# Loads of b issued from ScalarE's queue in a batched matrix product

## The chip, the cores and the metric

The kernel runs on one core of a Trainium2 chip. The time is device time in microseconds of one execution; the median over runs counts. The core has five engines that each take their instructions in order: PE (TensorE, matmuls and transposes), DVE (VectorE), ACT (ScalarE), POOL (GpSimd) and SP (SyncE). Transfers between HBM and on-chip memory are started by an instruction in the stream of one of these engines and carried out by the core's 16 DMA engines, while the engine that started them goes on. Where an instruction has to wait for something, all that stands behind it in the same engine's stream waits with it.

## The reference

```python
batch, m, k, n = 16, 512, 512, 512
a: (batch, m, k) float32      b: (batch, n, k) float32
return np.matmul(a, b.transpose(0, 2, 1)).astype(np.float32)
```

For each of 16 batches, out = a times b transposed, all 512 by 512 in float32. Each matrix is 1 MiB: the kernel must read 32 MiB and write 16 MiB.

## The kernel before

The function `load` (lines 43 to 48) brings in one batch: all of a[i] in one DMA (L46) and all of b[i] in another (L47). Each lays a matrix on 128 partitions, four whole rows on each, 8 KiB in one piece per partition. Six buffers exist for a and six for b. The loads of the first five batches are issued ahead of the loop (AHEAD = 5).

The loop then does the following for each batch i, in this order:

- `halve` (L52): VectorE casts a, then b, from float32 to bf16, one instruction each.
- `turn` (L62, L67): TensorE transposes the 128 by 128 blocks of the bf16 matrix, 16 for a and 16 for b, into PSUM, in groups of eight; each group is copied to SBUF by one instruction, so two copies a matrix. For a the copies run on ScalarE, for b on VectorE.
- `multiply` (L75, L80): for each of four row blocks, TensorE adds up four matmuls of 128 by 128 by 512 in PSUM, and ScalarE copies the block to the output tile `o_sb`, of which there are five buffers.
- `store` (L87): one DMA of 1 MiB writes the output of the batch.
- `load` of batch i + 5, as long as there is one.

All DMAs are started by SP, in program order: ten loads, then store 0, a5, b5, store 1, a6, b6, and so on to store 10, a15, b15, and then stores 11 to 15. The block stands under `tc.manual_schedule()`: each engine's stream has the order of the program text. The language's tile layer puts in all waits: for data, for a buffer to come free, and for the completion counters of the DMAs. So a store waits in SP's stream for ScalarE's last copy of the batch, and the loads behind it in the text wait with it.

ScalarE's stream holds, for each batch, the two copies of the transposed a and then the four copies of the output.

Of the kernel before, what the change touches and what calls it, by code (L numbers as in the profile page):

```python
# [1 line left out]

# [5 lines left out]


@with_exitstack  # L10
def kernel(
    ctx: ExitStack,
    tc: tile.TileContext,
    a: bass.AP,
    b: bass.AP,
    out: bass.AP,
):
    nc = tc.nc
    P = 128
    batch, M, K = a.shape  # L20
    _, N, _ = b.shape
    J = M // P
    KO = K // P
    f32 = mybir.dt.float32
    bf16 = mybir.dt.bfloat16
    AHEAD = 5

    const = ctx.enter_context(tc.tile_pool(name="ident", bufs=1))
    ident = const.tile([P, P], bf16)
    make_identity(nc, ident)  # L30

    apool = ctx.enter_context(tc.tile_pool(name="a_pool", bufs=6))
    bpool = ctx.enter_context(tc.tile_pool(name="b_pool", bufs=6))
    hpool = ctx.enter_context(tc.tile_pool(name="h_pool", bufs=2))
    tpool = ctx.enter_context(tc.tile_pool(name="t_pool", bufs=2))
    opool = ctx.enter_context(tc.tile_pool(name="o_pool", bufs=5))
    tppool = ctx.enter_context(tc.tile_pool(name="tp_pool", bufs=4, space=bass.MemoryType.PSUM))
    ppool = ctx.enter_context(tc.tile_pool(name="p_pool", bufs=4, space=bass.MemoryType.PSUM))

    def load(i):
        a_sb = apool.tile([P, J, K], f32, tag="a")
        b_sb = bpool.tile([P, J, K], f32, tag="b")
        nc.sync.dma_start(a_sb[:], a[i].rearrange("(p j) k -> p j k", j=J))  # L46
        nc.sync.dma_start(b_sb[:], b[i].rearrange("(p j) k -> p j k", j=J))  # L47
        return a_sb, b_sb

    def halve(src, tag):  # L50
        half = hpool.tile([P, J, K], bf16, tag="h" + tag)
        nc.vector.tensor_copy(out=half[:], in_=src[:])  # L52
        return half

    def turn(half, tag, copy):

        turned = tpool.tile([P, KO, J * P], bf16, tag="t" + tag)
        for ko in range(0, KO, 2):
            tp = tppool.tile([P, 2, J * P], bf16, tag="tp")
            for h in range(2):  # L60
                for j in range(J):
                    nc.tensor.transpose(  # L62
                        tp[:, h, j * P:(j + 1) * P],
                        half[:, j, (ko + h) * P:(ko + h + 1) * P],
                        ident[:],
                    )
            copy(out=turned[:, ko:ko + 2, :], in_=tp[:])  # L67
        return turned

    def multiply(aT, bT):  # L70
        o_sb = opool.tile([P, J, N], f32, tag="o")
        for j in range(J):
            ps = ppool.tile([P, N], f32, tag="p")
            for ko in range(KO):
                nc.tensor.matmul(  # L75
                    ps[:], aT[:, ko, j * P:(j + 1) * P], bT[:, ko, :],
                    start=(ko == 0), stop=(ko == KO - 1),
                )

            nc.scalar.copy(  # L80
                out=o_sb[:, j, :].rearrange("m (p j) -> m p j", j=J),
                in_=ps[:].rearrange("m (j p) -> m p j", j=J),
            )
        return o_sb

    def store(i, o_sb):
        nc.sync.dma_start(out[i].rearrange("(p j) n -> p j n", j=J), o_sb[:])  # L87

    loaded = {}
    with tc.manual_schedule():  # L90
        for i in range(min(AHEAD, batch)):
            loaded[i] = load(i)
        for i in range(batch):
            a_sb, b_sb = loaded.pop(i)
            a_h = halve(a_sb, "a")
            b_h = halve(b_sb, "b")
            aT = turn(a_h, "a", nc.scalar.copy)
            bT = turn(b_h, "b", nc.vector.tensor_copy)
            o_sb = multiply(aT, bT)
            store(i, o_sb)  # L100
            if i + AHEAD < batch:
                loaded[i + AHEAD] = load(i + AHEAD)


# [1 line left out]
_INS = ['a', 'b']  # L106
_OUTS = [((16, 512, 512), 'float32')]


# [23 lines left out]
```

## Time and profile before

| | |
|---|---|
| median of 7 runs | 126.63 us (126.42 to 126.82) |
| profiled execution | 126.72 us |
| its span, first to last instruction | 124.8 us |
| busy: TensorE | 92.2 us |
| busy: ScalarE | 68.4 us |
| busy: VectorE | 59.2 us |
| moved | 50.46 MB, mean 404 GB/s |
| HBM read, written | 33.55 MB, 16.78 MB |
| one 1 MiB DMA, issue to landing, median | 19.6 us |

How to read the lines that follow. On the page, the span is cut into 40 equal slices of 3.12 us; a digit is the busy share of a slice in tenths, and the row GB/s is what the DMA engines moved in it. A line of the waits reads: engine and line, what it waited for, then the total in us, the number of times and the longest. "SPq" is the stream of SP, which starts the DMAs. A line of a timeline reads: start in us, duration in us, engine, line, operation, out<-in, number of instructions merged, and in brackets the idle time before it and what ended that. A line of the chain reads: start, duration, what. A line of the windows reads: the stretch, its length, busy time and instructions of PE, PEld (weight loads), DVE, ACT and POOL, the granted TensorE clock, the DMA engines' busy share and GB/s.

### The profile page before, as it was taken

To read this page: it belongs to the slowest core of one execution; us is meant where nothing else is said; L and a number is where in the kernel's file an instruction comes from. 1 tells how busy PE (TensorE), PEld (TensorE's weight loads), DVE (VectorE), ACT (ScalarE), POOL (GpSimd) and SP (SyncE) were. 2 spreads that over 40 slices of the span, in tenths; PEclk is the share of its full clock that TensorE was granted. 3 is DMA by queue.
4 is the path that set the end of the run, shared out by engine and by line. 5 is a ranking of instruction groups with operands and counts; after the bars stand their busy time and mean duration, and the time that the engine had idled before them with its cause. 6 is when DMAs were issued, how large, how long until landed. Compare 5 with 4: busy or idle time off the path is not lost.

```text
span 124.8 us, 1885 instructions
## 1 busy us (share of the span) xinstructions
PE 92.2 (74%) x754; PEld 55.8 (45%) x768; DVE 59.2 (47%) x64; ACT 68.4 (55%) x97; POOL 0.7 (1%) x6
## 2 busy tenths in 40 slices
PE   0069989898989878949586794958769495886900
PEld 0056465655647445534534453444445344444300
DVE  0256555647373564474446537444653645456000
ACT  4041576777768683745738275582826649173610
POOL 2000000000000000000000000000000000000000
PEclk9999999999999999999999999999999999999995
DMA  3999999989999999999999999999999999999982
GB/s 100 425 425 425 423 436 420 412 326 415 436 431 423 423 420 425 436 423 420 425 423 428 428 431 412 423 428 431 428 428 412 428 425 431 428 423 417 417 347 116
DMA packets 6921, 50.46 MB, mean 404 GB/s; under 512 B 768, under 2 KB 768, under 8 KB 768
## 3 DMA queue, kind: packets, MB, share of 16 engines
q1 hardware_dynamic: 6912, 50.33, 96.5%
q8 instruction: 6, 0.10, 0.3%
q14 instruction: 3, 0.02, 0.0%
HBM read 33.55 MB, written 16.78 MB: 403 GB/s over the span
## 4 chain that ended last, share of the span: by engine, by line
DMA 80%; DVE 6%; PE 5%; SPq 3%; issue 1%; ACT 0%; DVEq 0%
DMA b_sb<-in_b_dram 80%; DVE half L52 4%; PE ps L75 3%; PE tp L62 2%; DVE turned L67 2%; SPq L46 1%; SPq L47 1%; ACT o_sb L80 0%; DVEq L52 0%
## 5 line engine op out<-in xcount | busy, mean ns | idle before, releaser
L75 PE MATMUL ps<-turned 128*128 128x512 bf16 x242 | 59.8, 382 | 6.1 <-DVE turned L67 5.5
L80 ACT COPY o_sb<-ps 128x512 f32<-128x512 f32 x64 | 37.5, 586 | 44.0 <-PE ps L75 40.8
L62 PE MATMUL tp<-ident,half 128*128 128x128 bf16 x512 | 34.8, 225 | 20.1 <-DVE half L52 20.1
L62 PEld LDWEIGHTS <-half 128*128 128x128 bf16 x512 | 31.3, 101 | 25.6 <-DVE half L52 24.1
L75 PEld LDWEIGHTS <-turned 128*128 128x128 bf16 x256 | 25.0, 98 | 36.5 <-issue 10.7
L67 ACT COPY turned<-tp 128x1024 bf16<-128x1024 bf16 x32 | 30.8, 1015 | 5.9 <-PE tp L62 5.9
L52 DVE CAST half<-a_sb 128x2048 bf16<-128x2048 f32 x16 | 19.6, 1224 | 22.1 <-DMA a_sb<-in_a_dram 22.1
L67 DVE COPY turned<-tp 128x1024 bf16<-128x1024 bf16 x32 | 20.7, 686 | 19.2 <-PE tp L62 19.2
L52 DVE CAST half<-b_sb 128x2048 bf16<-128x2048 f32 x16 | 19.6, 1226 | 14.7 <-DMA b_sb<-in_b_dram 14.7
L67 ACT ACT_TABLE_LOAD x1 | 1.3, 1283 | 0.7 <-PEq L117 0.7
masks.py:199 POOL TENSOR_SCALAR_AFFINE_SELECT ident<-ident 128x128 bf16<-128x128 bf16 x1 | 0.3, 294 | 0.1
masks.py:197 POOL MEMSET ident<- 128x128 bf16 x1 | 0.2, 205 | 0.3 <-POOLq L117 0.3
L117 POOL MEMSET const-bfloat16-1.0<- 128x1 bf16 x1 | 0.1, 102 | 0.0
L117 POOL MEMSET const-uint8-127<- 128x1 uint8 x1 | 0.1, 102 | 0.0
L117 POOL MEMSET const-float32-0.0<- 128x1 f32 x1 | 0.1, 99 | 0.2 <-issue 0.2
L117 POOL MEMSET const-float32-1.0<- 128x1 f32 x1 | 0.1, 99 | 0.0
## 6 DMA issues: line engine op xcount, KB each, us to landing
a_sb<-in_a_dram SPq DMA_DIRECT2D x16, 1024.0 KB, 19.6
b_sb<-in_b_dram SPq DMA_DIRECT2D x16, 1024.0 KB, 19.6
out_dram<-o_sb SPq DMA_DIRECT2D x16, 1024.0 KB, 19.6
```

Of the source, the lines that this page charges most:

```text
L46: nc.sync.dma_start(a_sb[:], a[i].rearrange("(p j) k -> p j k", j=J))
L47: nc.sync.dma_start(b_sb[:], b[i].rearrange("(p j) k -> p j k", j=J))
L52: nc.vector.tensor_copy(out=half[:], in_=src[:])
L62: nc.tensor.transpose(tp[:, h, j * P:(j + 1) * P], half[:, j, (ko + h) * P:(ko + h + 1) * P], ident[:],)
L67: copy(out=turned[:, ko:ko + 2, :], in_=tp[:])
L75: nc.tensor.matmul(ps[:], aT[:, ko, j * P:(j + 1) * P], bT[:, ko, :], start=(ko == 0), stop=(ko == KO - 1),)
L80: nc.scalar.copy(out=o_sb[:, j, :].rearrange("m (p j) -> m p j", j=J), in_=ps[:].rearrange("m (j p) -> m p j", j=J),)
L117: nc = _bacc.Bacc("TRN2", target_bir_lowering=False, num_devices=1)
```

## The change

The load of b is started by ScalarE instead of SP. The loads of a and the stores stay on SP.

```diff
     def load(i):
         a_sb = apool.tile([P, J, K], f32, tag="a")
         b_sb = bpool.tile([P, J, K], f32, tag="b")
         nc.sync.dma_start(a_sb[:], a[i].rearrange("(p j) k -> p j k", j=J))
-        nc.sync.dma_start(b_sb[:], b[i].rearrange("(p j) k -> p j k", j=J))
+        nc.scalar.dma_start(b_sb[:], b[i].rearrange("(p j) k -> p j k", j=J))
         return a_sb, b_sb
```

In ScalarE's stream the starts of b0 to b4 stand first, ahead of any copy. After that, the start of b(i+5) stands behind the four output copies of batch i and ahead of the two copies of the transposed a of batch i + 1. In SP's stream each load of a follows directly on the store of the batch, and the next store directly on that.

## The prediction

> **What bounds the kernel now.** I read the page's slices first, then the SP queue's waits, the timeline of SP's issues, ScalarE's timeline, and the windows of the end. The slices:
>
> ```profile
> span 124.8 us, 1885 instructions
> PE 92.2 (74%) x754; PEld 55.8 (45%) x768; DVE 59.2 (47%) x64; ACT 68.4 (55%) x97; POOL 0.7 (1%) x6
> DMA  3999999989999999999999999999999999999982
> GB/s 100 425 425 425 423 436 420 412 326 415 436 431 423 423 420 425 436 423 420 425 423 428 428 431 412 423 428 431 428 428 412 428 425 431 428 423 417 417 347 116
> ```
>
> The transfers bound it: full from the second slice to the last but one. 48 transfers of 1.049 MB at 426 GB/s (the window from 60 to 90 us) take 2.46 us each, 118 us in all. One batch is three transfers, 7.36 us. Next, what SP waits for, and its issues:
>
> ```profile
> SPq L87 <- DMA a_sb<-in_a_dram: 22.7, 11, 2.1
> SPq L46 <- DMA b_sb<-in_b_dram: 18.7, 9, 2.4
> SPq L47 <- DMA out_dram<-o_sb: 18.5, 9, 2.1
> ...
> 5.56 0.33 SPq L46 DMA_DIRECT2D a_sb<-in_a_dram  x1
> 8.08 0.33 SPq L47 DMA_DIRECT2D b_sb<-in_b_dram  x1
> ...
> 72.64 0.34 SPq L87 DMA_DIRECT2D out_dram<-o_sb  x1
> ...
> 92.26 0.33 SPq L47 DMA_DIRECT2D b_sb<-in_b_dram  x1
> ```
>
> Each issue waits for a landing. Call a0, b0, s0 the transfers of batch 0. In program order they are a0 b0 ... a4 b4, then s0 a5 b5, s1 a6 b6, up to s10 a15 b15, then s11 to s15. The ninth issue (a4) starts at 5.56, when a0 lands; the tenth (b4) at 8.08, when b0 lands. b15 starts at 92.26, 19.62 us after s8's issue at 72.64; the median from issue to landing is 19.6. So every transfer waits for the one eight places earlier: a store for an a, a load of a for a b, and **a load of b for the store of two batches before** (b15 for s8, b14 for s7). That is the third line above. Today only SP stands in these waits, and nothing but DMA issues is queued behind them.
>
> ScalarE, and the end:
>
> ```profile
> 39.22 0.59 ACT L80 COPY o_sb<-ps 128x512 f32<-128x512 f32 x1 [0.28 <-PE ps L75]
> 39.72 1.93 ACT L67 COPY turned<-tp 128x1024 bf16<-128x1024 bf16 x2
> ...
> 45.12 0.59 ACT L80 COPY o_sb<-ps 128x512 f32<-128x512 f32 x1 [0.28 <-PE ps L75]
> ...
> 81.58 0.59 ACT L80 COPY o_sb<-ps 128x512 f32<-128x512 f32 x1 [0.28 <-PE ps L75]
> 82.08 1.93 ACT L67 COPY turned<-tp 128x1024 bf16<-128x1024 bf16 x2
> ...
> 114.61 0.59 PE ps L75 x2
> ...
> 118.43 0.59 ACT o_sb L80
> ```
>
> With the data there, a batch takes 5.90 us (39.22 to 45.12, last copies of two batches); TensorE sets that. From a batch's first matmul to its last copy's end it is 4.41 us (114.61 to 119.02). Batch 10 is finished at 82.17, ten microseconds before b15 can be issued, and ScalarE goes straight on to batch 11. That free run is what the change touches. At the end, s15 is issued at 119.02 and the span ends 5.78 us later.
>
> **The change, part by part.** *Removed from SP:* 16 issues of 0.33 us, 5.3 us. SP is no engine of the chain except in the first 4.3 us, where it issues faster than the transfers run; worth nothing.
>
> *The start.* a0 and b0 are issued together. If the queues share the transfers equally, a0 lands with b0 near 8.1 instead of 5.57, and the first products come up to 2.5 us later (nothing, if a0 keeps its place). b4, the tenth transfer, holds ScalarE until b0 lands; the table load of 1.28 us may follow it, while a0 is cast (1.23) and transposed. None of it reaches the end: batches 0 to 5 run at 5.90 against transfers at 7.36 and are ahead for good. I take 0.
>
> *Added to ScalarE:* 16 issues, bounded by SP's rows at 0.33 to 0.91 us. Five come before any work. ScalarE is busy 68.4 of 124.8 us, so the others cost nothing by themselves, except the one in the sum below.
>
> *The wait that moves.* ScalarE takes its instructions in order. The load of b(k+5) stands behind batch k's copies and ahead of batch k+1's two copies of turned a. I take the count of eight to run on in program order over both queues: the profile names a landing as releaser, so the program puts the wait there, not a full queue. Then ScalarE stands until s(k-2) has landed; behind it are turned a of batch k+1, the matmuls that need it, the next store, and behind that store on SP the next load of a. TensorE and VectorE can only prepare one batch.
>
> From its release a batch takes 0.33 (issue) + 1.02 (first turned copy, mean 1015 ns) + 4.41 = 5.8 us. Stores land every 7.36 us while the transfers are full. So in the steady state ScalarE waits about 1.5 us in each batch, the transfers stay full (when s8 lands s9, s10, a14, a15 and others are outstanding), and the page would look alike. But the computing now trails: batch 10 ends 1.5 us before b15's issue instead of ten before.
>
> *The end pays for it.* Call T the issue of b15. Batches 11 to 15 are all still to be computed: 5.8 for batch 11, 4 x 5.90 for 12 to 15 with the operands there, then 5.78 for the last store. Span = T + 5.8 + 23.6 + 5.8 = T + 35.2. After T at most twelve transfers are left, 29.5 us, so these are no longer the limit: the transfers run dry between the last stores.
>
> T is the landing of s8. Served in program order that is 92.26 as now. With its own queue, b13 and b14 (the only later loads of b that can be issued without s8) can pass s8, each 2.46 us: T to 97.2. The other way, b12 could fall behind s8: T = 89.8. I take one passed, 94.7, because the b queue holds fewer transfers than the other and so is drained ahead. Span 94.7 + 35.2 = 129.9. The profiled execution took 126.72 with a span of 124.8, so 1.92 lie around it: 131.8. The median of the runs is 126.63, 0.09 lower: **131.7 us**. The ends: T = 89.8 gives 126.8, program order (92.26) 129.3, two passed 134.2.
>
> The share between the queues is in no row of this trace. The Trainium skill, page "DMA: Bandwidth & Descriptors", section "Queues, rings and completion order", says each DMA engine takes turns between the queues it has work for, packet by packet. By that rule b, a third of the traffic, gets up to half of the service while it has work; both b13 and b14 would pass and the sum would be 134.2 instead of 131.7.
>
> A rule speaks against any effect. SP's issues take 5.3 us of a span of 124.8, and the transfers run at 426 GB/s already. The same page, section "Issuing engines are not separate DMA queues", says that starting transfers from several engines only saves the sequencer's issue time. By that rule the time stays 126.6; it counts neither the wait that travels with the issue nor the order.
>
> **The rivals.**
> *Each queue counts its own eight.* Then b(k+5) waits for a load of b that landed long ago and ScalarE is hardly held. For it: in the trace one queue and one count can't be told apart. Against: the releaser is a landing, as above. The loads of b run ahead, and a15 comes last, behind s10, at 111.8 as b15 does now. Where a13, a14 and a15 follow each other 4.9 us apart (one store between), a13 lands at 102.0; batch 13 takes 7.2 from its last operand as batch 15 does now (111.83 to 119.02), so 109.2, then 2 x 5.90 and 5.8: span 126.8, time 128.6. Without that bunching 126.6, and with a further batch behind 131.
>
> *Faster: the second queue fills gaps of the first.* Between 25 and 30 us the rate is 360, 311, 311, 377 and 410 GB/s, 0.86 us of lost transfer, though eight are outstanding:
>
> ```profile
> 25.00:26.00 1.00, 1.00 (x7) 0.46 (x5) 1.00 (x2) 0.72 (x2) 0.00 (x0) 1.00 0.90 360
> 26.00:27.00 1.00, 1.00 (x6) 0.41 (x5) 0.42 (x1) 0.72 (x2) 0.00 (x0) 1.00 0.91 311
> 27.00:28.00 1.00, 1.00 (x16) 0.87 (x15) 0.00 (x0) 0.72 (x3) 0.00 (x0) 1.00 0.87 311
> 28.00:29.00 1.00, 1.00 (x21) 1.00 (x19) 0.24 (x1) 1.00 (x3) 0.00 (x0) 1.00 0.89 377
> ```
>
> A second queue with work would give 125.8; at the best slice's 436 GB/s throughout another 2.7, 123.1. It decides only if ScalarE isn't held, that is if s(k-2) lands before batch k's last copy; now s8 lands ten microseconds after that of batch 10.
>
> *No effect.* The transfers' order and the lag cancel: s8 served early and batch 11 released with it, T = 89.8 (126.8). It needs b12 late without the batches waiting for it; they would.
>
> *The change doesn't split the transfers*: both engines' issues served strictly in program order. ScalarE is held all the same; 129.3, inside the forecast.
>
> **How the numbers follow.** ScalarE held, 0.81: 131.7, from 129.3 to 134.2, and beyond where ScalarE's wait also keeps SP's loads of a back and the transfers thin out before T. Own eight, 0.09: 128.6. Faster, 0.06. No effect, 0.04. The range 127.8 to 135.4 leaves out the two last cases and a tenth of the first. Runs of before spread over 126.42 to 126.82, so 0.2% is about what can be told. Slower: 0.81 and nearly all of 0.09, 0.89; same 0.05; faster 0.06.
>
> **What would show it.** Right: waits of ScalarE's queue for out_dram at the load of b, about 1.5 us a batch; loads of b that land sooner than 19.6 us, a and stores no sooner than about 16; b15 issued near 95; the last five batches 5.9 us apart; GB/s falling to about a 1 MB store per 5.9 us, 180, in the last three or four slices; a0's cast starting near 8. Wrong: no wait of ScalarE's queue, or one under 0.5 us, makes it the second or third case; slices over 430 GB/s throughout, the third; a last stretch that is full of transfers, that T + 35.2 isn't the end.

## The result, and the profile after

The change makes the kernel slower: 128.34 us, the median of 12 runs (127.80 to 129.69), against 126.71 us (31 runs of the kernel before, 126.33 to 127.04). The ratio is 1.0148, with a 95% interval of 1.0125 to 1.0171. The direction and the range of the forecast hold; the size does not: 5 us more were forecast, 1.6 came.

The page of the changed kernel, its span, the clock and transfer slices and the DMA issues:

```profile
span 126.0 us, 1877 instructions
...
PEclk9999999999999995996799999599999999999999
DMA  4999999999999999999999999999999999999825
GB/s 86 419 426 424 424 429 419 416 369 424 426 424 432 421 424 421 434 429 419 413 419 424 424 432 424 421 413 429 421 426 432 421 419 424 439 421 424 367 125 229
...
b_sb<-in_b_dram ACTq DMA_DIRECT2D x16, 1024.0 KB, 11.5
a_sb<-in_a_dram SPq DMA_DIRECT2D x16, 1024.0 KB, 21.6
out_dram<-o_sb SPq DMA_DIRECT2D x16, 1024.0 KB, 17.6
```

The transfers run at the same rate as before, and as full, up to slice 37 (slices are counted from 0). The new thing is a hole near the end: 125 GB/s in slice 38, then 229. And the three kinds of transfer, whose median was 19.6 us from issue to landing, have come apart: b takes 11.5, a 21.6, a store 17.6.

What SP and ScalarE now wait for:

```profile
SPq L87 <- DMA a_sb<-in_a_dram: 63.5, 11, 8.9
SPq L87 <- ACT o_sb L80: 23.6, 6, 6.8
```

```profile
ACT L67 <- DMA b_sb<-in_b_dram: 8.8, 1, 8.8
ACT turned L67 <- DMA out_dram<-o_sb: 5.8, 2, 2.9
```

ScalarE is held, as forecast: at the start for b0, and later by the landing of stores. SP's waits for landings were spread over three places of a batch before (22.7 us at stores, 18.7 at loads of a, 18.5 at loads of b); now they fall on its stores, 63.5 us, which wait for loads of a, and the next load of a stands behind the store. ScalarE's timeline shows one long wait at a load of b (b13) and the last one (b15) with next to none:

```profile
73.79 0.59 ACT L80 COPY o_sb<-ps 128x512 f32<-128x512 f32 x1 [0.27 <-PE ps L75]
76.78 0.34 ACTq L47 DMA_DIRECT2D b_sb<-in_b_dram  x1
77.21 1.93 ACT L67 COPY turned<-tp 128x1024 bf16<-128x1024 bf16 x2 [2.83 <-DMA out_dram<-o_sb]
...
89.54 0.59 ACT L80 COPY o_sb<-ps 128x512 f32<-128x512 f32 x1 [0.28 <-PE ps L75]
90.23 0.33 ACTq L47 DMA_DIRECT2D b_sb<-in_b_dram  x1
```

The chain that ends last comes out of a load of a. The piece that starts at 79.64 is a13, and nothing of ScalarE's queue is in what follows. The first line is from the kernel before, where the chain comes out of b15:

```profile
92.26 19.57 DMA b_sb<-in_b_dram
```

```profile
79.64 21.59 DMA a_sb<-in_a_dram
...
102.46 1.23 DVE half L52
...
105.14 0.59 PE ps L75 x2
...
111.05 0.59 PE ps L75 x2
...
116.94 0.59 PE ps L75 x2
...
120.76 0.59 ACT o_sb L80
```

After a13 three batches follow, their first matmuls 5.9 us apart (105.14, 111.05, 116.94). The windows show the hole that this leaves before the last store; the first two lines are from the kernel before:

```profile
112.00:118.00 6.00, 4.40 (x30) 2.41 (x32) 2.44 (x3) 3.08 (x5) 0.00 (x0) 1.00 1.00 419
119.00:124.80 5.80, 0.00 (x0) 0.00 (x0) 0.00 (x0) 0.01 (x1) 0.00 (x0) 0.76 0.55 229
```

```profile
110.00:118.00 8.00, 7.27 (x65) 4.45 (x64) 4.85 (x6) 5.57 (x8) 0.00 (x0) 1.00 1.01 422
118.00:120.00 2.00, 1.95 (x10) 0.93 (x10) 0.00 (x0) 1.28 (x3) 0.00 (x0) 1.00 0.72 303
120.00:122.00 2.00, 0.72 (x4) 0.11 (x2) 0.00 (x0) 1.07 (x2) 0.00 (x0) 1.00 0.03 12
122.00:126.00 4.00, 0.00 (x0) 0.00 (x0) 0.00 (x0) 0.00 (x0) 0.00 (x0) 1.00 0.64 262
```

Issue and landing of single transfers can be read from the trace's records of the completion counters. Those of the last batches, in us from the start of the span:

| | before | changed |
|---|---|---|
| a0, b0 land | 5.55, 8.06 | 8.24, 8.44 |
| s7 lands, s8 lands | 84.8, 92.2 | 90.2, 98.8 |
| b15 is issued | 92.26 | 90.23 |
| a13, a14, a15 land | 94.6, 102.0, 109.4 | 101.2, 106.1, 111.0 |
| b13, b14, b15 land | 97.1, 104.5, 111.8 | 87.5, 92.9, 99.2 |
| last copy of batch 10 ends | 82.2 | 90.1 |
| last copy of batch 15 ends | 119.0 | 121.3 |

Up to 118 us the transfers are full in both kernels. What differs is whose they are: b14 and b15 have landed before a13. In the kernel before the pairs come 7.4 us apart and one batch is left to compute when the last has landed; in the changed kernel batch 13 gets its pair at 101.2, 14 and 15 theirs 4.9 us apart, faster than the 5.9 us that a batch takes, and the last batches queue up behind TensorE.

a13 lands 6.6 us later than before. It is issued 4.6 us later (79.64 against 75.05), because SP stands at s8 until a10 has landed at 79.14 (72.58 in the kernel before), although batch 8's last copy ended at 74.4; and it is under way for 21.59 us instead of 19.59. The lag is older than the end: a7 landed at 57.03 instead of 50.44, 6.6 us late already.

### The profile page after: what moved, and what is told of

It is laid out like the page before. It is cut to its first block, busy times and chain, and to the rows that moved or that the text cites. A ratio compares the mean times of both kernels' runs of the same rounds, so it can differ in the third digit from the quotient of the medians.

```text
span 126.0 us, 1877 instructions
## 1 busy us (share of the span) xinstructions
PE 94.8 (75%) x754; PEld 56.4 (45%) x768; DVE 57.9 (46%) x64; ACT 68.9 (55%) x97; POOL 0.7 (1%) x6
## 4 chain that ended last, share of the span: by engine, by line
DMA 72%; PE 17%; DVE 4%; issue 2%; SPq 1%; ACT 0%; DVEq 0%
DMA a_sb<-in_a_dram 58%; DMA b_sb<-in_b_dram 14%; PE ps L75 11%; PE tp L62 6%; DVE turned L67 2%; DVE half L52 2%; SPq L87 1%; ACT o_sb L80 0%; SPq L46 0%; DVEq L67 0%; DVEq L52 0%
## 5 line engine op out<-in xcount | busy, mean ns | idle before, releaser
L75 PE MATMUL ps<-turned 128*128 128x512 bf16 x242 | 64.0, 402 | 15.3 <-ACT turned L67 10.5
L62 PE MATMUL tp<-ident,half 128*128 128x128 bf16 x512 | 33.0, 225 | 10.5 <-DVE half L52 10.4
L52 DVE CAST half<-a_sb 128x2048 bf16<-128x2048 f32 x16 | 19.6, 1223 | 27.1 <-DMA a_sb<-in_a_dram 27.1
## 6 DMA issues: line engine op xcount, KB each, us to landing
b_sb<-in_b_dram ACTq DMA_DIRECT2D x16, 1024.0 KB, 11.5
a_sb<-in_a_dram SPq DMA_DIRECT2D x16, 1024.0 KB, 21.6
out_dram<-o_sb SPq DMA_DIRECT2D x16, 1024.0 KB, 17.6
```

The source lines that it names most:

```text
L62: nc.tensor.transpose(tp[:, h, j * P:(j + 1) * P], half[:, j, (ko + h) * P:(ko + h + 1) * P], ident[:],)
L75: nc.tensor.matmul(ps[:], aT[:, ko, j * P:(j + 1) * P], bT[:, ko, :], start=(ko == 0), stop=(ko == KO - 1),)
```

## The experiments

Two theories were put against each other. **H**, the forecast's: the end is set by ScalarE, which stands at a load of b until a store has landed. **Q**: the end is set by the order of service; on a queue of its own, b is served ahead of a, and the last loads of a come late.

### Queue without a held ScalarE

```diff
-        nc.scalar.dma_start(b_sb[:], b[i].rearrange("(p j) k -> p j k", j=J))
+        nc.gpsimd.dma_start(b_sb[:], b[i].rearrange("(p j) k -> p j k", j=J))
```

> All loads of b are issued from GpSimd, which does nothing else, so ScalarE's stream holds no load; the loads of b still run on a queue of their own beside the loads of a and the stores. Theory H (the end is set by ScalarE standing at the load of b until a store has landed): the loss is gone, 126.2 to 127.3 us. Theory Q (the end is set by the order of service: with b on its own queue b14 and b15 are served ahead of a13, so the last loads of a come late and three batches are still to be computed after a13): the loss stays, 127.8 to 129 us, with a13 landing near 101 as in the changed kernel (94.6 before). If loads of b from GpSimd take much longer than 11 us to land, neither is tested.

130.21 us, 1.0267 (1.0251 to 1.0282). The loss doesn't go, it grows, beyond the bands of both theories. GpSimd issues b as soon as a buffer is free, so b runs further ahead: b15 is issued at 79.4 and lands at 90.0, and a takes up to 34.8 us. The chain, where the second piece is a11, landing at 91.7 with five batches still to come:

```profile
32.40 24.58 DMA a_sb<-in_a_dram
57.05 34.62 DMA a_sb<-in_a_dram
```

Loads of b took 24.6 us in the median, not about 11, since up to six of them stand in their own queue at once; a13 landed at 101.45. ScalarE waited for no transfer in this run. So loads of b on another queue cost with ScalarE free. But loads that take 24.6 us are the case in which the expectation calls neither theory tested, and the run changes one thing more: eleven loads were issued before the first landing (a0 at 5.63), so GpSimd's loads are counted apart from SP's, and SP's transfers wait for others than in the changed kernel. That a held ScalarE limits the loss in the changed kernel, since it keeps b from running further ahead, fits these numbers and was not tested by itself.

### No wait at the load of b, with both queues

```diff
-        nc.sync.dma_start(out[i].rearrange("(p j) n -> p j n", j=J), o_sb[:])
+        o = out[i].rearrange("(p j) n -> p j n", j=J)
+        for j in range(0, J, 2):
+            nc.sync.dma_start(o[:, j:j + 2, :], o_sb[:, j:j + 2, :])
```

> The changed kernel with each store cut in two halves of 512 KB, both issued after the batch's last copy. A batch then has four transfers and eight back from a load of b is the load of b two batches before, which has landed, so ScalarE is no longer held; the two queues stay. Theory H: as fast as the kernel before with the same cut store, within 0.4 us. Theory Q: still 1.2 to 2.5 us slower than that one.

> The kernel before with the same cut store: the control of the run with the changed kernel. Both theories: 125.5 to 127.0 us; the last store's two halves land at most 1.2 us earlier than one whole store, if the transfers have room, and otherwise nothing changes.

With the cut store the changed kernel takes 129.46 us (1.0214, 1.0195 to 1.0233) and the kernel before 127.80 (1.0076, 1.0061 to 1.0091): 1.66 us between them, where H allowed 0.4 and Q 1.2 to 2.5. ScalarE was held in the loop once, for 4.1 us, by a load of b. The chain comes out of a12, under way for 17.41 us from 79.64 and landing at 97.05 (87.50 in the control), with four batches behind it, so a13's landing at 102.0 no longer decided. The control was itself 1.0 us slower than the kernel before, which neither theory had: its last copy ends at 119.3 instead of 119.0, and the halves of the last stores land later. Why was not looked into.

### A held ScalarE with one queue

```diff
-    opool = ctx.enter_context(tc.tile_pool(name="o_pool", bufs=5))
+    opool = ctx.enter_context(tc.tile_pool(name="o_pool", bufs=3))
```

> The kernel before with three output buffers instead of five. ScalarE's first output copy of batch k then waits for the store of batch k-3 to land; in the kernel before s7 lands at 84.8 us and batch 10's first copy is at 79.0, so ScalarE is held some 4 to 6 us a batch, with all transfers still in one queue. Theory H: a held ScalarE alone makes the computing trail and costs 2 to 4 us, 128.7 to 130.7. Theory Q: the order of service is as before, and it costs 0 to 0.6 us, 126.5 to 127.3.

128.81 us, 1.0191 (1.0137 to 1.0246): inside H's band, outside Q's, though ScalarE was held 3.4 us a batch in the mean and not 4 to 6. ScalarE's total of waits, and the end of the chain:

```profile
ACT o_sb L80 <- DMA out_dram<-o_sb: 37.9, 11, 3.5
```

```profile
94.68 19.56 DMA out_dram<-o_sb
114.25 0.02 issue
...
114.81 1.57 ACT o_sb L80 x3
116.38 0.34 ACT turned L67
...
121.50 0.59 ACT o_sb L80
```

The loads land where they did (a13 at 94.6, b15 at 111.8), and yet batch 15 ends at 122.1: batch 14's copies wait for s11, and the turned a of batch 15 stands behind them. So a held ScalarE costs as well, where the hold reaches to the end. In the changed kernel it doesn't: ScalarE's last long wait is that for b13, at 76.8. H is a real mechanism and not the one that sets this end.

### Less passing

Loads of b three batches ahead instead of five, first from ScalarE, then from GpSimd with three buffers:

```diff
+    B_AHEAD = 3
...
-        nc.scalar.dma_start(b_sb[:], b[i].rearrange("(p j) k -> p j k", j=J))
+    def load_b(i):
+        b_sb = bpool.tile([P, J, K], f32, tag="b")
+        nc.scalar.dma_start(b_sb[:], b[i].rearrange("(p j) k -> p j k", j=J))
+        return b_sb
...
             if i + AHEAD < batch:
                 loaded[i + AHEAD] = load(i + AHEAD)
+            if i + B_AHEAD < batch:
+                loaded_b[i + B_AHEAD] = load_b(i + B_AHEAD)
```

> The changed kernel, but the loads of b run three batches ahead instead of five; a stays at five. ScalarE still stands at each load of b for the store of three batches before the one just finished. Theory Q (order of service): the loads of b no longer pass the loads of a by much, the last loads of a land within 3 us of the kernel before (a13 at 94.6, a15 at 109.4), and the loss goes: 126.3 to 127.3 us. Theory H (ScalarE held): the wait is the same, so 128 us or more.

> Loads of b from GpSimd with three buffers of b instead of six, so that they can run at most three batches ahead. ScalarE's stream holds no load. Theory Q: with less passing, most of the 3.4 us that loads of b from GpSimd with six buffers cost are gone: 126.5 to 128.0 us. If the passing isn't the cause but the queue itself (slower transfers, worse mixing), 130 us as before.

From ScalarE 126.40 us, 0.9981 (0.9948 to 1.0014), eight of ten runs from 126.07 to 126.66 and two at 127.45 and 127.83; from GpSimd 127.14 us, 1.0021 (1.0006 to 1.0036) instead of 1.0267. Both as Q has it. With three ahead a13 lands at 96.4 and a15 at 111.1. The loss of the changed kernel is gone though ScalarE is held as long as in it (5.9 us in two waits for stores, 5.8 there), and though SP waits as long at its stores for loads of a (67.3 us, 63.5 there), so that the loss doesn't follow from how long either of them waits. Here H does set the end: the chain runs through ScalarE's queue at b14, held until s8 has landed at 93.9, and from there through batches 12 to 15.

```profile
74.32 19.57 DMA out_dram<-o_sb
93.89 0.03 ACTq L51
...
93.96 0.34 ACTq L51
```

### Only the last loads in turn

```diff
-        nc.scalar.dma_start(b_sb[:], b[i].rearrange("(p j) k -> p j k", j=J))
+        (nc.sync if i >= 13 else nc.scalar).dma_start(b_sb[:], b[i].rearrange("(p j) k -> p j k", j=J))
```

> The changed kernel with b13, b14 and b15 issued from SP again, b0 to b12 from ScalarE. Theory Q: only what is served ahead of a13 to a15 counts at the end; these three now come in turn, and the time is 126.4 to 127.2 us though ScalarE has been held in the middle. If the lag of the middle is never made up, 128 us or more.

> As with the last three loads of b on SP, but the last five (b11 to b15). Theory Q: it makes no difference from when on the last loads come in turn, as long as a13 to a15 aren't passed: 126.0 to 126.7 us, as with three. If what is gained over the kernel before comes from the loads of b on ScalarE, fewer of them give it back: 126.7.

(For five, 11 in place of 13.) 126.33 us, 0.9953 (0.9926 to 0.9980), and 126.30 us, 0.9957 (0.9938 to 0.9975). Three loads put back into turn take away the whole loss and leave 0.4% to 0.5% of gain: the fastest kernels of this study. ScalarE's waits for b9 and b10 stay (5.2 us with three, 5.6 with five), its wait for b13 goes with the load, so these two runs don't by themselves tell Q from H. They do show that a lag in the middle costs nothing if it is gone at the end: a7 is as late as in the changed kernel (57.1 with three, 56.8 with five), but a13 lands at 93.9 and 94.0. With three, the last load of b lands at 111.1 instead of 111.8, and the chain ends through it as in the kernel before:

```profile
91.55 19.60 DMA b_sb<-in_b_dram
111.14 0.03 issue
...
117.74 0.59 ACT o_sb L80
```

Where these 0.7 us come from was not settled.

### The start

```diff
+        (nc.sync if i < 5 else nc.scalar).dma_start(b_sb[:], b[i].rearrange("(p j) k -> p j k", j=J))
```

> The changed kernel with b0 to b4 issued from SP, in turn with a0 to a4, and b5 to b15 from ScalarE. My step that the start is worth nothing: as the changed kernel within 0.6 us, 127.7 to 129 us, though a0 lands near 5.6 us again instead of 8.2. If the start counts, up to 1.5 us faster than the changed kernel.

128.77 us, 1.0157 (1.0120 to 1.0193), with a0 landing at 5.57. The start is worth nothing that shows, as the forecast took it. a13 lands at 101.9 and the last copy ends 20.1 us later, the same 20.1 us as in the changed kernel.

### Both remedies, put together wrongly

Loads of b three ahead, and `(nc.sync if i >= 13 else nc.scalar)`:

> Both remedies together: loads of b three batches ahead, b13 to b15 from SP, the others from ScalarE. In the run with three ahead alone the chain of the end starts at ScalarE's load of b14, held until s8 landed at 93.9 us, and T plus the last four batches set the end. Theory Q with H as a second limit: neither passing nor a held ScalarE is left at the end, the last load of b lands near 111 us, and the time is 125.8 to 126.5 us, at most 0.7% faster than the kernel before, since the transfers are full to 118 us in either. If there is a third limit, 126.5 us or more.

134.15 us, 1.0571 (1.0541 to 1.0601), the opposite of what I expected. Three ahead on SP means that b13 stands behind s10 and a15 in the queue:

```profile
89.13 0.33 SPq L46
...
89.51 16.82 DMA b_sb<-in_b_dram
106.34 0.03 issue
```

It lands at 106.3, and the last copy ends 20.8 us after it, the same tail once more. A miss of the edit. It shows the second half of Q, what one late operand of batch 13 costs with three batches of compute behind it, and not the first: b13 was late by its place in SP's own queue, not because another queue was served ahead of it.

## Why the prediction was right or wrong

**What bounds the kernel.** Right. The transfers do, at the same rate in both kernels, and the loss is a hole in them at the end (12 GB/s from 120 to 122 us).

**The start, and SP's issues: nothing.** Right for the start, by the run with the first five on SP. What SP's saved issues are worth was not tested by itself.

**The count of eight runs on over both queues.** Right: b4's issue at 8.46 follows b0's landing at 8.44 and holds ScalarE at the start. The rival that each queue counts its own eight falls with it.

**"In program order", a load of b for the store of two batches before.** Wrong, and this is the step that failed first. In the changed kernel a load of b has its turn ahead of the store of its batch, not behind it, and so waits for the store of *three* batches before. b15 was issued at 90.23, 0.07 us after s7 landed at 90.16; s8 landed at 98.76. The other loads of b agree (b9 0.08 us after s1, b10 0.08 after s2, b13 0.10 after s5). The text has the load behind the store and the load of a; the turns of the built program have it ahead of both, presumably because on ScalarE it no longer stands behind SP's store. A kernel with two queues that counts in text order was not tried.

**T = 94.7.** Mis-sized by 4.5 us: 90.2 measured. Two errors met in it. The store was the wrong one (s7 lands 7.4 us before s8 in the kernel before), and one passed transfer was too little: s7 landed 5.35 us later than before, 2.2 transfers.

**A wait of 1.5 us in each batch.** Wrong in shape. From batch 2 on the waits were 2.5 us (b9), 1.9 (b10), 2.4 (b13) and at most 0.7 elsewhere, 7.6 us over the nine loads b7 to b15, where 1.5 each would be 13.5. The store waited for had mostly landed before ScalarE came to the load. What was late was a, behind stores on SP that waited for earlier loads of a. That queue behind a slower a was not in the forecast's steady state.

**Span = T + 35.2.** The length is right, 35.8 measured (126.0 less 90.2), but not its cause, so that it fits is luck. ScalarE stood only 0.1 us at b15, whose issue came right after batch 10's last copy (90.12). Batch 11 took 6.2 instead of 5.8, the four after it 24.9 instead of 23.6, the last store 4.7 instead of 5.8. The 1.3 us too many stand at batch 13, whose a was not there: "with the operands there" failed. The end adds up from a13 without any wait of ScalarE: a13 at 101.2, 8.3 to batch 13's last copy, 2 x 5.9, 4.7, which is 126.0. In span the forecast was 3.9 us too long (129.9), 4.5 by T less 0.6 by what follows.

**The transfers run dry between the last stores.** Only before the very last: they were full to 118 us, as the windows show. The forecast had named a last stretch full of transfers as the sign that T + 35.2 isn't the end, and so it was.

**The rivals.** The sum of the first one (a13 at 102.0, batch 13 finished at 109.2, span 126.8) is nearly what happened (101.2, 109.55, 126.0). I had tied it to a condition that isn't needed, that each queue counts for itself, and gave it 0.09. Passing was enough, with one count for both queues. The gap between 25 and 30 us shrank (slice 8 from 326 to 369 GB/s) and did not save the changed kernel.

**The two rules that were weighed.** That the queues are served in turn, packet by packet (the Trainium skill, "DMA: Bandwidth & Descriptors", "Queues, rings and completion order"), agrees with this trace: a0 and b0, issued together, land at 8.24 and 8.44, where one queue had them at 5.55 and 8.06. The working from it had two transfers pass s8; s8 landed 6.6 us later than before, 2.7 transfers, and s7, the one that counted for b15, 2.2. That several issuing engines only save issue time (same page, "Issuing engines are not separate DMA queues") agrees in the rate (slices of 413 to 439 GB/s against 412 to 436, but for the dip near 27 us and the ends), and not in the time: the order of service moved the end by 1.2 us of span with the same 48 transfers.

## What to carry to other kernels

In this kernel, bound by transfers, a second queue moved no byte faster, but it changed which operand lands last and how much work then stands behind it. In such a case forecast the end from the landing of each of the last operands, and add the compute of every batch that still waits for one. Here the stream that had a queue to itself ran ahead of its partner, which shared one with the stores (11.5 us from issue to landing against 21.6). What removed the loss was to give it a shorter lead, or to put its last few loads back into the partner's queue, in turn. And before a wait is priced, find out which earlier transfer it is for, since moving one issue to another engine can change the turn of all of them.

## What had not been expected of the hardware

TensorE's granted clock fell to 0.5 for 3.4 us three times in the changed kernel, each time after TensorE had stood still for 2.82, 2.25 and 2.74 us while ScalarE was held (PEclk shows it as 5 to 7 in slices 15, 18 and 19, and 25; mean clock 0.959 against 0.989). The window around the first, where the third number from the end is that clock:

```profile
46.00:52.50 6.50, 5.64 (x25) 2.44 (x27) 2.36 (x2) 3.28 (x6) 0.00 (x0) 0.74 1.01 425
```

Batch 5 took 7.9 us from its release to its last copy instead of 5.8. In the kernel before, with idle stretches of 1.3 us, it stayed at full speed to 122 us. Length alone doesn't decide: with three output buffers TensorE stood still for 1.46 to 1.48 us in most batches, and the clock fell after one of these stretches, at 81.8 us, and not after the others. The lower clock doesn't set the end here: the runs with the last loads of b on SP have a mean clock of 0.967 and 0.964 and are the fastest.
